# A store of 512 bytes a partition beside the first load of a split-GELU-multiply kernel

## The chip, the cores and the metric

The kernel runs on one core of a Trainium2 chip. The metric is the device time of one execution in microseconds (us); less is better. All runs quoted here are fast: one core, granted clock 1.0, no run over 1.5% above the fastest of its kernel. A ratio is the mean time of one kernel's fast runs over the mean of the other's in the same rounds, so it isn't quite the ratio of the medians that stand beside it. "Clear" below means that the 95% interval of that ratio leaves out 1.

## The reference

The input is 32 x 512 rows of 2048 float32 numbers. Each row is cut in two halves; GELU of the first half is multiplied by the second.

```python
def setup_inputs():
    batch, seq, dim = (32, 512, 2048)
    return {'x': np.random.randn(batch, seq, dim).astype(np.float32)}

def reference(x):
    half_dim = x.shape[-1] // 2
    x1, x2 = (x[..., :half_dim].copy(), x[..., half_dim:].copy())
    gelu_x1 = 0.5 * x1 * (1 + erf(x1 / np.sqrt(2)))
    return (gelu_x1 * x2).astype(np.float32)
```

That is 134.22 MB to read and 67.11 MB to write, and little arithmetic.

## The kernel before

Sixteen tiles of 128 partitions x 8 rows. A load brings 65,536 contiguous bytes to each partition, in one packet each (the trace has 2,048 packets of that size for 16 loads of 128 partitions); a store takes 32,768 from each (1,920 packets for the fifteen whole ones). Loads are issued on SyncE's queue, two tiles ahead; stores on ScalarE's queue, but for the last tile, whose store goes out in four pieces on SyncE's queue.

```python
    xpool = ctx.enter_context(tc.tile_pool(name="xpool", bufs=2))
    opool = ctx.enter_context(tc.tile_pool(name="opool", bufs=2))

    def load(i):
        x_tile = xpool.tile([P, R, dim], x.dtype, name="x_tile")
        nc.sync.dma_start(out=x_tile, in_=x_t[i])
        return x_tile

    ahead = [load(0), load(1)]
    for i in range(n_tiles):
        # ... GELU on ScalarE (in place), multiply on VectorE, row by row ...
            queue = nc.sync if last else nc.scalar
            queue.dma_start(out=o_t[i][:, rows, :], in_=o_tile[:, rows, :])
        if i + 2 < n_tiles:
            ahead.append(load(i + 2))
```

## Time and profile before

| | before |
|---|---|
| median time, first three runs | 472.24 us (471.88 to 472.30) |
| span of the profiled run | 470.3 us |
| VectorE / ScalarE busy | 31% / 26% |
| bytes moved, mean rate | 201.35 MB, 428 GB/s |

The lines of this profile, and how they are read, are in the prediction. Its result: some 6 us of the span are not explained by the bytes.

One source is used below that the summary page doesn't show: the trace's record of every DMA packet, with its queue, start, size and duration, though not which of the 16 engines carried it. From it I use one derived figure throughout, the **excess**. A packet of 65,536, 32,768 or 8,192 bytes normally takes 2.42, 1.213 or 0.309 us. What packets take beyond that (counted from 0.02 us on) is summed over a stretch and divided by 16; it is the mean time that an engine lost there. No view prints these records; every excess below was counted from them, in one trace of each kernel. "Stall" below means the excess at the first large store, 1.19 us in the kernel before.

### The profile page before, as it was taken

To read this page: it belongs to the slowest core of one execution; us is meant where nothing else is said; L and a number is where in the kernel's file an instruction comes from. 1 tells how busy PE (TensorE), PEld (TensorE's weight loads), DVE (VectorE), ACT (ScalarE), POOL (GpSimd) and SP (SyncE) were. 2 spreads that over 40 slices of the span, in tenths; PEclk is the share of its full clock that TensorE was granted. 3 is DMA by queue.
4 is the path that set the end of the run, shared out by engine and by line. 5 is a ranking of instruction groups with operands and counts; after the bars stand their busy time and mean duration, and the time that the engine had idled before them with its cause. 6 is when DMAs were issued, how large, how long until landed. Compare 5 with 4: busy or idle time off the path is not lost.

```text
span 470.3 us, 408 instructions
## 1 busy us (share of the span) xinstructions
DVE 146.7 (31%) x128; ACT 124.2 (26%) x129; POOL 0.2 (0%) x4
## 2 busy tenths in 40 slices
DVE  0070704307042070520606116060250702407034
ACT  1050605106050150601406024060330603206042
POOL 0000000000000000000000000000000000000000
DMA  8999999999999999999999999999999999999998
GB/s 357 446 446 382 429 443 424 463 404 443 426 446 421 443 415 449 413 443 424 457 429 435 438 438 415 426 438 435 440 440 418 449 438 435 424 443 432 418 410 351
DMA packets 5042, 201.35 MB, mean 428 GB/s; under 512 B 560, under 2 KB 560, under 8 KB 560
## 3 DMA queue, kind: packets, MB, share of 16 engines
q1 hardware_dynamic: 2880, 138.41, 68.4%
q10 hardware_dynamic: 2160, 62.92, 31.0%
q14 instruction: 2, 0.02, 0.0%
HBM read 134.22 MB, written 67.11 MB: 428 GB/s over the span
## 4 chain that ended last, share of the span: by engine, by line
DMA 81%; DVE 15%; ACT 2%; DVEq 0%; issue 0%; SPq 0%; ACTq 0%
DMA x_tile<-in_x_dram 81%; DVE o_tile L55 15%; ACT x_tile L52 2%; DVEq L90 0%; SPq L40 0%; ACTq L52 0%
## 5 line engine op out<-in xcount | busy, mean ns | idle before, releaser
L55 DVE TENSOR_TENSOR o_tile<-x_tile 128x1024 f32<-128x1024 f32 x128 | 146.7, 1218 | 316.8 <-ACT x_tile L52 316.8
L52 ACT ACTIVATE x_tile<-x_tile 128x1024 f32<-128x1024 f32 x128 | 122.9, 1042 | 336.0 <-DMA x_tile<-in_x_dram 336.0
L52 ACT ACT_TABLE_LOAD x1 | 1.3, 1283 | 0.7 <-PEq L79 0.7
L79 POOL MEMSET const-bfloat16-1.0<- 128x1 bf16 x1 | 0.1, 102 | 0.0
L79 POOL MEMSET const-uint8-127<- 128x1 uint8 x1 | 0.1, 102 | 0.0
L79 POOL MEMSET const-float32-1.0<- 128x1 f32 x1 | 0.1, 99 | 0.0
L79 POOL MEMSET const-float32-0.0<- 128x1 f32 x1 | 0.1, 98 | 0.2 <-issue 0.2
## 6 DMA issues: line engine op xcount, KB each, us to landing
out_dram<-o_tile ACTq DMA_DIRECT2D x15, 4096.0 KB, 39.4
out_dram<-o_tile SPq DMA_DIRECT2D x4, 1024.0 KB, 5.6
x_tile<-in_x_dram SPq DMA_DIRECT2D x16, 47.6
```

The source lines that it names most:

```text
L52: nc.scalar.activation(out=x_tile[:, r, :half], in_=x_tile[:, r, :half], func=GELU)
L55: nc.vector.tensor_mul(out=o_tile[:, r, :], in0=x_tile[:, r, :half], in1=x_tile[:, r, half:],)
L79: nc = _bacc.Bacc("TRN2", target_bir_lowering=False, num_devices=1)
```

## The change

The intent, as far as the code shows it, is to use ScalarE's queue once, early, so that the first real store finds it in use. The bytes written are dummies, and the last piece of the last store overwrites them.

```diff
+    first = ctx.enter_context(tc.tile_pool(name="first", bufs=1)).tile([P, 1, 128], out.dtype)
+    nc.vector.memset(first, 0.0)
+    nc.scalar.dma_start(out=o_t[n_tiles - 1][:, R - 1 :, half - 128 :], in_=first)
 
     ahead = [load(0), load(1)]
```

## The prediction

> **What bounds the kernel now.** I read the page first: busy shares, then the 40 slices, then the bytes.
>
> ```profile
> span 470.3 us, 408 instructions
> ...
> DVE 146.7 (31%) x128; ACT 124.2 (26%) x129; POOL 0.2 (0%) x4
> ...
> DMA  8999999999999999999999999999999999999998
> GB/s 357 446 446 382 429 443 424 463 404 443 426 446 421 443 415 449 413 443 424 457 429 435 438 438 415 426 438 435 440 440 418 449 438 435 424 443 432 418 410 351
> ...
> HBM read 134.22 MB, written 67.11 MB: 428 GB/s over the span
> ```
>
> No compute engine passes 31%, while the DMA row is at 9 in all but its first and last slice. The 16 DMA engines are the bound, and the bytes are given by the problem (134.22 MB in, 67.11 MB out). Next I read the chain that ended last:
>
> ```profile
> 1.16 45.96 DMA x_tile<-in_x_dram
> ...
> 57.44 47.69 DMA x_tile<-in_x_dram
> ...
> 115.50 47.63 DMA x_tile<-in_x_dram
> ...
> 173.50 47.63 DMA x_tile<-in_x_dram
> ...
> 405.50 47.65 DMA x_tile<-in_x_dram
> ```
>
> The columns are start, duration, what. Each link is a load's wait plus one tile's compute, and the links start exactly 58.0 us apart (57.44, 115.50, 173.50). Two tiles are 2 x (8.39 + 4.19) = 25.17 MB, and 25.17 MB / 58.0 us is 434 GB/s. So the compute inside each link is not what paces it: loads are queued two deep, and the transfers run through it. At that rate all 201.33 MB take 464.0 us. The span is 470.3, so everything that can be gained without moving fewer bytes is some 6 us, 1.3%. That alone almost excludes "faster by over 2%".
>
> Where are these 6 us? By the DMA queue's record of single packets, the first starts at 1.75 us and the last store's completions end at 469.0: 1.75 + 1.3 us lie outside, about 3.2 us inside. I looked for stretches under 434 GB/s in the view of engine time by stretch (stretch, length, busy us of DVE, ACT, POOL, clock, DMA share, GB/s):
>
> ```profile
> 34.00:41.60 7.60, 0.00 (x0) 0.00 (x0) 0.00 (x0) 1.00 1.00 366
> 41.60:57.40 15.80, 9.16 (x8) 7.68 (x8) 0.00 (x0) 1.00 1.01 438
> 57.40:86.40 29.00, 9.11 (x9) 7.68 (x8) 0.00 (x0) 1.00 1.00 434
> ...
> 458.00:469.00 11.00, 5.49 (x5) 2.91 (x4) 0.00 (x0) 1.00 0.92 379
> ```
>
> The first line is the interesting one. From 34 us the engines are fully occupied (share 1.00) and move 366 GB/s: they lose (1 - 366/434) x 7.6 = 1.19 us. It comes right behind the first store, issued on ScalarE's queue at 32.93. The packet records agree: a 65,536-byte load packet takes 2.42 us everywhere, but 23 of them between 34.1 and 39.0 us take 2.98 to 3.60, an excess of 18.8 us in sum, 1.17 us for each of 16 engines. The second store, at 57.44, and those after it show nothing of the kind. Something in the first store costs 1.17 us, once; this is evidently what the change aims at. Two other slow places stand beside it. The first packet of each engine takes 0.1 to 1.0 us more than 2.42 (mean 0.57). At 458 us, where stores begin on the load queue after it has run dry, 8 engines' first packets take 0.7 to 1.1 us more.
>
> [...]here load packets (65,536 bytes) and store packets (32,768 bytes) do alternate, so the added store takes time from the first load and not from idle hardware. [...]the added store has just 512 a partition, and no transfer of that size is in this trace. [...]
>
> **The change part by part.** It removes nothing. It adds:
>
> 1. A memset of 128x1x128 f32 on VectorE, at about 0.75 us. VectorE is idle until 23.7, so even a few tenths of a microsecond cost nothing.
> 2. One DMA issue on ScalarE. An issue there takes 0.36 us (median in the store's line). ScalarE has only its table load (0.72 to 2.00 us) to do before 22.64, so even with the wait for the memset this is hidden:
>
> ```profile
> 0.72 1.28 ACT L52 ACT_TABLE_LOAD   x1 [0.72 <-PEq L79]
> 0.73 0.86 SPq L40 DMA_DIRECT2D x_tile<-in_x_dram  x2
> ```
>
> 3. Its bytes: 128 x 512 = 65.5 KB, 8 packets for each engine. From the records, 8,192 bytes take 309 ns and 32,768 take 1,213, so a byte costs 0.0368 ns and a packet 8 ns besides; 512 bytes then take an estimated 27 ns, eight of them 0.21 us. These are engine time on the bound, so they count in full: +0.2 us.
> 4. A dependence: the last quarter of the last store overwrites these bytes and must wait for the small store. That one is issued at 463.5 us and the small one is done by about 20 (one small packet behind each of the first load's eight packets of 2.42 us). Cost 0. The shift of semaphores by one transfer shouldn't add a wait either, for neighbours keep their distance.
> 5. What it moves: if the 1.17 us is a cost of the queue's first store on each engine, the real first store no longer pays it, but the small one does, at 2 to 6 us, while the first load runs. There it costs the bound as much as before, except for what hides behind the first load's own slow start (mean 0.57 us of excess in the same first packets). The small store's descriptors should reach the engines roughly 1 us after its issue (as the first load's did: issue 0.73, first packet 1.75), hence at about 2.0 us, just as those slow packets are under way.
>
> Sum if it warms: -1.17 + 0.21 + a repeated stall of 0 to 1.17. That is -0.96 to +0.21, middle -0.4 us.
>
> **The rivals.** First rival: the stall isn't first use but the waking of an empty queue. For it: the second store came while the first was still under way (the first landed at 66.7, the second was issued at 57.44), so the trace has no second waking of ScalarE's queue; and the load queue, sixteen loads old, shows slow packets at 458 when it wakes. Against it: those eight engines had probably just finished everything else, so an empty pipeline explains them as well. If it holds, the small store is over by 20 us, the queue is empty at 32.9, the old stall stays and a second one may come: +0.2 to +1.4, middle +0.8 us.
>
> Second rival: it's the turn from reading alone to reading and writing. Then 64 KB of writes at 3 us train nothing, the stall at 34 stays, and only the 0.2 us of packets is added, with perhaps tenths for eight small turns an engine: +0.2 to +0.6.
>
> Third rival: a wait. If the program were to order the large stores behind the small one, because they go to the same tensor, the first store at 32.9 would still find it landed at 20. No effect. Only if such a wait sat on SyncE ahead of the first load, or if ScalarE held its table load until after 22 us, would it show; both are placed on other queues or over long before.
>
> **Range and chances.** I give warming 0.5, the two rivals that keep the stall 0.25 each. The mean is 0.5 x (-0.4) + 0.25 x 0.8 + 0.25 x 0.4 = +0.1 us, so I predict no more than a nudge: 472.24 + 0.1 - 0.2 for the chance of fully hiding the repeated stall is 472.1. The edges: the best case is -0.96, the worst +1.4, and the three runs before span 0.42 us. So 470.9 to 473.5 should hold it 8 times in 10. Two per cent are 9.4 us, over one and a half times all that is lost today; I leave 0.01 for faster and 0.01 for slower (a wait I overlooked), 0.98 for the same.
>
> **What would show each step.** In the changed profile: a row for the small store among the DMA issues, x1, 64 KB, with 15 to 20 us to landing (packet-by-packet alternation; a landing of 3 us would refute that). The stretch from 34.0 to 41.6 us at about 434 GB/s and the load packets there at 2.42 us if warming holds; still 366 if a rival does. The first load's packets at 2 to 6 us lengthened if the stall moved. The chain's links still 58.0 us apart. The landing of the second load, 47.13 before, shows the balance by itself: 46.2 to 47.3 with warming, 47.3 to 48.5 without; the end of the span should move by the same amount. The prediction is wrong if the links' spacing changes, if a wait on the small store shows up in the chain, or if the end moves by over 1.5 us.

That 434 GB/s can't be passed, on which the 6 us rest, is an estimate from this trace, which held that rate from link to link, 58.0 us at a time; it was not shown.

## The result, and the profile after

After: 472.38 us median (472.26 to 472.67, 4 runs). Before: 472.27 us (471.88 to 472.57, 4 runs). The ratio is 1.0004, with a 95% interval of 0.9986 to 1.0021: the same.

The page of the changed kernel, its busy shares and bytes:

```profile
span 470.6 us, 411 instructions
...
DVE 146.9 (31%) x129; ACT 124.2 (26%) x129; POOL 0.2 (0%) x4
...
HBM read 134.22 MB, written 67.17 MB: 428 GB/s over the span
```

There are three instructions more and 0.06 MB more written; the busy times agree within 0.2 us. The start of the timeline (start, duration, engine, line, what, and in brackets the idle time before it):

```profile
0.73 57.39 SPq L40 DMA_DIRECT2D x_tile<-in_x_dram  x4
0.83 0.17 DVE L45 MEMSET first<- 128x128 f32 x1 [0.83 <-PEq L84]
1.02 0.42 ACTq L46 DMA_DIRECT2D out_dram<-first  x1
1.47 1.28 ACT L57 ACT_TABLE_LOAD   x1 [1.47 <-DVE first L45]
22.93 7.68 ACT L57 ACTIVATE x_tile<-x_tile 128x1024 f32<-128x1024 f32 x8 [20.18 <-DMA x_tile<-in_x_dram]
```

The memset, the issue and the delayed table load are over by 2.75 us and ScalarE then waits 20.18 us for the first load, so these three are hidden. But the first load is in at 22.93; before, ScalarE could start at 22.64. That is +0.29 us on the bound. The chain that ended last (start, duration, what) carries it on:

```profile
1.17 46.31 DMA x_tile<-in_x_dram
...
57.79 47.68 DMA x_tile<-in_x_dram
...
115.84 47.64 DMA x_tile<-in_x_dram
...
405.85 47.64 DMA x_tile<-in_x_dram
```

The second load ends at 47.48 (1.17 + 46.31) in place of 47.13, the next links start 0.35 us later than before (57.79 against 57.44), the spacing is still 58.0 us, and the last link is 0.35 us later too (405.85 against 405.50). So what happened, happened before 58 us and wasn't given back. These are single traces, and 0.35 us is less than the 0.7 us over which the four runs of the kernel before spread.

Did the first store's stall go away? The view by stretch seems to say yes and then no:

```profile
34.00:41.60 7.60, 0.00 (x0) 0.00 (x0) 0.00 (x0) 1.00 1.16 431
34.30:41.90 7.60, 0.00 (x0) 0.00 (x0) 0.00 (x0) 1.00 0.97 354
```

Both lines are of the changed kernel. The first is the stretch that read 366 GB/s before; it now reads 431. Moved by 0.3 us, the amount by which everything came later, it reads 354. This view books a packet's bytes where the packet starts; packets are 2.4 us long and start in bunches, so an edge that cuts a bunch was worth 77 GB/s here. A DMA share of 1.16, over 1, is the sign of it. The packet records settle it: between 34.2 and 38.8 us, 19 load packets took 3.06 to 3.65 us in place of 2.42, an excess of 1.22 us an engine, against 1.17 (1.19 by the same count) before. The stall stayed in full.

The small store itself, in the view of DMA issues (what, queue, times, KB each, us from issue to landing):

```profile
out_dram<-first ACTq DMA_DIRECT2D x1, 64.0 KB, 24.3
```

Its packets are in the records: 128 of 512 bytes at 27 ns, alternating with the load's, the first at 7.21 us. Eight for each engine make 0.21 us, and the first packets of the first load have 0.66 us of excess in place of 0.57. 0.21 + 0.09 is the 0.3 us by which the first load is late. But the 0.09 is within chance: in the runs below whose first packets meet nothing new (e4_s7, e10_skew32 to e13_skew_ports) the same excess is 0.60 to 0.76.

### The profile page after: what moved, and what is told of

Read it like the earlier page. It is cut to its first block, busy times and chain, and to the rows that moved or that the text cites. A ratio compares the mean times of both kernels' runs of the same rounds, so it can differ in the third digit from the quotient of the medians.

```text
span 470.6 us, 411 instructions
## 1 busy us (share of the span) xinstructions
DVE 146.9 (31%) x129; ACT 124.2 (26%) x129; POOL 0.2 (0%) x4
## 4 chain that ended last, share of the span: by engine, by line
DMA 81%; DVE 15%; ACT 2%; DVEq 0%; issue 0%; SPq 0%; ACTq 0%
DMA x_tile<-in_x_dram 81%; DVE o_tile L60 15%; ACT x_tile L57 2%; DVEq L95 0%; SPq L40 0%; ACTq L57 0%
## 6 DMA issues: line engine op xcount, KB each, us to landing
out_dram<-first ACTq DMA_DIRECT2D x1, 64.0 KB, 24.3
```

## The experiments

Four theories were tested. (The expectations also say "ring", for the queue of one issuing engine.) **W**: the stall is the waking of an empty store queue. **T**: it is the turn from reading alone to reading with large stores. **F**, later **C**: it is paid once a run, by the first large store (F), or by whatever first crowds the engines (C). "Crowds" means here that something lengthens their packets, as the column "early" below counts it. **P**: it is the shock of 16 engines in step meeting large stores at once. The theory of the prediction, that a small first store warms the queue, had fallen with the profile after.

The table has all twelve runs beside the two kernels. "Early" is the excess an engine between 4 and 30 us, "first store" that between 30 and 60 us, where the first full-size store meets the loads.

| run | early | first store | median us | before in its rounds |
|---|---|---|---|---|
| before | 0.00 | 1.19 | 472.27 | |
| the change | 0.00 | 1.22 | 472.38 | 472.27 |
| e1_late | 0.03 | 1.13 | 473.59 | 472.37 |
| e2_bridge | 0.00 | 0.86 | 472.26 | 472.37 |
| e3_big | 1.37 | 0.00 | 473.64 | 472.37 |
| e4_s7 | 0.00 | 1.42 | 473.40 | 472.37 |
| e5_2k | 0.02 | 1.21 | 473.41 | 472.31 |
| e6_skew | 0.62 (and 2.59 before 4 us) | 0.00 | 474.88 | 472.31 |
| e7_sync | 0.88 | 0.11 | 473.65 | 472.31 |
| e8_8k | 0.05 | 1.27 | 472.88 | 472.31 |
| e10_skew32 | 3.36 | 0.00 | 475.84 | 472.39 |
| e11_drain | 0.00 | 1.31 | 473.14 | 472.39 |
| e12_half | 0.00 | 0.94 | 471.84 | 472.39 |
| e13_skew_ports | 0.00 | 1.33 | 473.48 | 472.48 |

All gave correct results.

**e1_late: the small store in the middle of the first load.**

```diff
-    nc.vector.memset(first, 0.0)
+    for _ in range(60):
+        nc.vector.memset(first, 0.0)
```

> The small store as in the change, but behind 60 memsets of its tile, so that it is issued some 7 to 10 us into the first load, when load packets run at their steady 2.42 us and no slow start hides anything. Theory W (waking an empty store queue stalls the loads): load packets lengthened by some 1.2 us for each engine just after the small store's descriptors arrive, the first load lands 1.2 us later than 22.93, and the old stall stays at 34 us; the time goes up by 1.0 to 1.3 us against the change. Theory T (the stall is the turn from reading alone to large stores beside the reads): no load packet lengthened at 10 us, the stall at 34 stays, first load lands at 22.9, the time is that of the change within 0.3 us.

The 60 memsets took longer than I thought; the small store was issued at 16.26 us. From its timeline:

```profile
0.82 15.41 DVE L46 MEMSET first<- 128x128 f32 x60 [0.82 <-PEq L85]
16.26 0.38 ACTq L47 DMA_DIRECT2D out_dram<-first  x1
22.69 7.68 ACT L58 ACTIVATE x_tile<-x_tile 128x1024 f32<-128x1024 f32 x8 [4.74 <-DMA x_tile<-in_x_dram]
```

The first load is in by 22.69 (before: 22.64), and no load packet was lengthened when the small store came. So small packets woke the queue without a loss (0.03 us of excess between 4 and 30 us), even where no slow start could hide it. More than that: the small store's last completions came at 38.7 to 40.1 us, so the queue was not empty when the first real store was issued at 32.98, and the stall came all the same, 1.13 us an engine between 38.7 and 40.1, the moment before the large packets began. W is out as the cause of this stall. The time is clearly longer (ratio 1.0026, 1.0011 to 1.0041), by 1.2 us against the change. That is the time W asked for, but not for W's reason, since neither the lengthened load packets nor the late first load came; T asked for no more than 0.3 us. The longer time shows at the end: 15 of the 16 last completions came by 468.75 us, earlier than before (469.00), and one at 470.50. With the extra instructions there was a third fetch of 8,192 bytes of program, at 27.09, and a load packet starting at 27.39 took 0.53 us more; the two fetches of the kernel before, at 180.09 and 198.32, each came with one lengthened load packet in the same way (0.24 and 0.53 us). That the late engine is the one that fetches is argued, not shown.

**e2_bridge: the small store lasts until the real one comes.**

```diff
-    first = ... .tile([P, 1, 128], out.dtype)
+    first = ... .tile([P, 2, 128], out.dtype)
-    nc.scalar.dma_start(out=o_t[n_tiles - 1][:, R - 1 :, half - 128 :], in_=first)
+    nc.scalar.dma_start(out=o_t[n_tiles - 1][:, R - 2 :, half - 128 :], in_=first)
```

> The small store has two pieces of 512 bytes a partition, 16 packets an engine in place of 8; at one packet behind each load packet of 2.42 us it lasts from 7 to some 45 us, so that the store queue is not empty when the first real store is issued at 33.2. Theory W: no stall of load packets at 34 to 39 us, none when the first large packets come at about 45 either; second load lands at about 46.7 (47.50 less 1.2, plus 0.2 for 8 more packets, with fewer large store packets ahead of it sooner still); end about 0.8 to 1.0 us earlier than the change, about 471.5. Theory T: the stall comes all the same, at 44 to 48 us, when the first large packets run; time 472.6, 0.2 over the change.

Small packets ran from 7.1 to 41.8 us, about one in every 2.4 us on each engine; the stall came at 41.3 to 41.8 us, on all 16 engines at once, 0.86 us each, as the first large packets were next. This is against W again. The time was the same (0.9998, 0.9983 to 1.0013).

**e3_big: one full-size packet an engine, early.**

```diff
-    first = ... .tile([P, 1, 128], out.dtype)
-    nc.vector.memset(first, 0.0)
-    nc.scalar.dma_start(out=o_t[n_tiles - 1][:, R - 1 :, half - 128 :], in_=first)
+    first = opool.tile([P, R, half], out.dtype, name="o_tile")
+    nc.vector.memset(first[:16], 0.0)
+    nc.scalar.dma_start(out=o_t[n_tiles - 1][:16], in_=first[:16])
```

> In place of the small store one full-size packet an engine: 16 partitions of 32,768 bytes, issued at about 9 to 10 us after a memset of 16x8192. It adds 0.52 MB, 1.21 us for each engine. Theory W and theory T both: load packets lengthened by about 1.2 us an engine at 10 to 15 us, and again at 34 to 39 us, as the queue is empty (W) and the engines read alone (T) again by then; first load lands at 22.6 + 1.2 + 1.2 = 25.0; end 2.4 us over before, 474.6. Theory F (only the first full-size store in the program pays): stall at 10 to 15, none at 34 to 39; end 1.2 us over before, 473.4.

Here the stall at the first real store is gone, while 1.37 us an engine were lost at 12 to 17 us. The time, 473.64, is what F asked for (473.4) and not what W and T asked for (474.6). By the view of stretches, from 29 to 49 us, this kernel first, then before:

```profile
29.00:49.00 20.00, 6.56 (x6) 4.67 (x6) 0.00 (x0) 1.00 1.03 444
```
```profile
29.00:49.00 20.00, 4.67 (x5) 3.18 (x4) 0.00 (x0) 1.00 1.02 416
```

(The view's weakness told above applies; the records have no load packet over 2.44 us in this stretch of e3_big.) T is out too in its plain form: the engines read alone from 20 us on and turned to mixing at 39 without a loss.

The records show that the early loss has another form than the stall, so it isn't shown to be the stall moved forward. In the ten kernels that stall (0.86 us or more in the table), load packets are lengthened, and at least 16 of them start before the first large store packet: in the kernel before 16 of 23, from 34.09 us, while the first store packet starts at 37.27; in e1_late and e2_bridge all 16. The first store packets themselves take their usual time. In e3_big the early store's own packets are lengthened (1.64 to 2.98 us in place of 1.213, 1.25 of the 1.37 us), and load packets hardly (0.13).

**e4_s7: ScalarE's queue runs dry in mid-run.** The kernel before, with one line changed:

```diff
-            queue = nc.sync if last else nc.scalar
+            queue = nc.sync if last or i == 7 else nc.scalar
```

> The kernel before (no small store), with the eighth tile's store issued on SyncE's queue in place of ScalarE's. ScalarE's queue then runs dry for some 20 us in the middle of the run, and is woken by the ninth tile's store; SyncE's queue goes from load packets to store packets and back in one ring without ever being empty. Theory W: load packets lengthened, about 1.2 us an engine, once more when the ninth tile's store arrives, and none where the eighth's begins; end about 1.2 us over before. Theory T: a stall where the eighth tile's store begins to run after a stretch of reading alone, if there is one, and none or the same at the ninth. Theory F: no stall besides the one at 34, time as before within 0.5 us unless the order of transfers in SyncE's queue delays a load.

On SyncE's queue the engines went from load packets straight to 10 us of store packets alone, at 245.3 us, and every one took 1.213 us, give or take 0.02: that turn cost nothing. When the ninth tile's store then woke ScalarE's queue, load packets between 258 and 265 us were lengthened by 0.5 us an engine, less than half of what W asked, and 0.1 came at 297. By the stretch from 258 to 267 us of this kernel (the kernel before has 419 GB/s there, and the view's weakness applies):

```profile
258.00:267.00 9.00, 0.00 (x0) 0.00 (x0) 0.00 (x0) 1.00 0.97 397
```

So something does come back here, in part, and it comes when a dry queue gets a large store, as W asks. A strict "once a run" isn't right either. The time is clearly longer (1.0022, 1.0007 to 1.0037), by 1.0 us where W asked for 1.2 and F for at most 0.5.

**e5_2k and e8_8k: how large must the early store be?** The change with 2,048 bytes a partition, and one packet of 8,192 bytes for each engine from 16 partitions:

```diff
 e5_2k
-    first = ... .tile([P, 1, 128], out.dtype)
+    first = ... .tile([P, 1, 512], out.dtype)
-    nc.scalar.dma_start(out=o_t[n_tiles - 1][:, R - 1 :, half - 128 :], in_=first)
+    nc.scalar.dma_start(out=o_t[n_tiles - 1][:, R - 1 :, half - 512 :], in_=first)
 e8_8k (against e3_big)
-    nc.vector.memset(first[:16], 0.0)
-    nc.scalar.dma_start(out=o_t[n_tiles - 1][:16], in_=first[:16])
+    nc.vector.memset(first[:16, :2], 0.0)
+    nc.scalar.dma_start(out=o_t[n_tiles - 1][:16, :2], in_=first[:16, :2])
```

> The change with 2,048 bytes a partition in place of 512: eight packets of an estimated 83 ns for each engine (0.0368 ns a byte and 8 ns), 0.67 us in all, one behind each packet of the first load. Theory F (the first large store pays the stall, once): if 2,048 bytes are large enough, load packets near 7 us are lengthened and those at 34 to 39 us are not; if not, the stall of 1.2 us an engine stays at 34 to 39. Time 472.4 + 0.46 = 472.9 if the stall only moves or stays. Theory P (the stall is the shock of 16 engines in step turning to large stores at once): stays at 34 to 39, same time.

> One early store packet of 8,192 bytes an engine on ScalarE's queue (16 partitions, memset of 16x2048, issue at about 4.5 us), 0.31 us of engine time. Theory F: an excess of 0.3 to 1.2 us an engine at 6 to 10 us and what is missing from 1.2 at 34 to 39, so that the sum stays about 1.2; time 472.3 + 0.3 = 472.6. Theory P: whatever happens at 6 to 10, the excess at 34 to 39 goes down as the first load's completions spread more.

Neither crowded the engines early (0.02 and 0.05) and neither took anything off the stall (1.21 and 1.27). For e8_8k no share of the 1.2 moved to the front, which is a miss of F as I had put it; nor did the excess at 34 to 39 us go down, which is a miss of P. Its time isn't clearly longer (1.0008, 0.9993 to 1.0023). e5_2k took 1.1 us more than before (1.0021, 1.0004 to 1.0038) where 0.6 was expected; its last completions are spread from 468.99 to 470.29.

**e6_skew and e7_sync.** No early store but an extra load of 8 partitions in front of the first; and the early full-size store on SyncE's queue:

```diff
 e6_skew (against before)
+    first = opool.tile([P, R, half], out.dtype, name="o_tile")
+    nc.sync.dma_start(
+        out=first[:8].rearrange("p (a b) d -> p a (b d)", b=2), in_=x_t[0][:8, : R // 2]
+    )
 
 e7_sync (against before)
-    ahead = [load(0), load(1)]
+    ahead = [load(0)]
+    first = opool.tile([P, R, half], out.dtype, name="o_tile")
+    nc.vector.memset(first[:16], 0.0)
+    nc.sync.dma_start(out=o_t[n_tiles - 1][:16], in_=first[:16])
+    ahead.append(load(1))
```

> No early store; in its place an extra load of 8 partitions x 32,768 bytes in front of the first load, which keeps 8 of the 16 engines busy 1.21 us longer, so that the engines no longer reach the first store in step (the completions of the first load spread over about 1.8 us in place of 0.6). Theory P: the excess at 34 to 39 us falls to half or less of the 1.2 us an engine. Theory F: it stays at 1.1 to 1.3 us an engine. The end is set by the 8 engines with more work: 472.3 + 1.2 = 473.5 with F, 472.5 to 472.9 with P.

> The full-size early store of 16 partitions x 32,768 bytes is put on SyncE's queue, between the first and the second load, so one store packet an engine runs at about 22 us in the ring of the loads. Theory F with the cost belonging to the engine or to the memory, not to the ring: an excess of about 1.2 us an engine at 20 to 24 us, none at 34 to 39; time 473.6 as with the full-size store on ScalarE's queue. If the cost belongs to the first large use of ScalarE's ring: no excess or the same at 22, and again 1.2 at 34 to 39; time 473.6 to 474.8. Theory P: a stall at 22, as the engines are in step, and little at 34 to 39.

e6_skew took the stall away without any early store, which spoke for P and against F. But it had a defect: the extra load lost 2.6 us an engine of its own in the first microseconds (2.59 + 0.62, less the usual 0.6), which I had not asked for. e7_sync lost 0.88 at 19 to 24 us on the loads' queue, 0.64 of it on the early store's own packets, and left 0.11 at the first real store. In both runs the first use of ScalarE's queue went almost without loss (0.00 and 0.11 us). So the cost doesn't belong to the first use of that queue.

**e10_skew32 and e13_skew_ports: the skew alone.** Both put the extra load of 8 x 32,768 bytes between the first and the second load. They differ only in the partitions it is written to:

```diff
 e10_skew32 (against before)
-    ahead = [load(0), load(1)]
+    ahead = [load(0)]
+    extra = opool.tile([P, R, half], out.dtype, name="o_tile")
+    nc.sync.dma_start(
+        out=extra[:8, : 2 * 4].rearrange("p (a b) d -> p a (b d)", b=2),
+        in_=x_t[1][:8, :4],
+    )
+    ahead.append(load(1))
 
 e13_skew_ports (against e10_skew32)
-        out=extra[:8, : 2 * 4].rearrange("p (a b) d -> p a (b d)", b=2),
+        out=extra[0:32:4, : 2 * 4].rearrange("p (a b) d -> p a (b d)", b=2),
```

> No early store. An extra load of 8 partitions x 32,768 bytes on 8 of the 16 engines stands between the first and the second load, so that the start is untouched and those engines come to the first store 1.21 us behind the others. Theory P (the stall is the shock of engines in step turning to large stores at once): excess at 34 to 39 us at most 0.3 us an engine, in place of 1.2. Theory C (a cost paid once a run, by the first thing that upsets the start, which the misplaced extra load of the run before this may have paid with its 2.6 us of added excess in the first microseconds): 1.1 to 1.3 us an engine at 34 to 39. The end: 8 engines have 1.21 us more to do, so 472.3 with P (1.2 added, 1.2 saved), 473.5 with C.

> The extra load of 8 x 32,768 bytes between the first and the second load again, but written to partitions 0, 4, 8 ... 28 in place of 0 to 7. [...]extra packets at about 1.21 us, load packets at 2.42, and the 8 engines are simply 1.21 us behind the others. Then the run tells the two theories apart, for nothing but the skew is left. Theory P (engines in step): excess at 34 to 39 us at most 0.3 us an engine, end near 472.3. Theory C (a stall paid once a run, by whatever first crowds the engines: in all the runs without it at 34, something had crowded them before): 1.1 to 1.3 us an engine at 34 to 39, end near 473.5.

The stretch from 21.6 to 29 us, first of e10_skew32, then of e13_skew_ports:

```profile
21.60:29.00 7.40, 4.68 (x5) 5.76 (x7) 0.00 (x0) 1.00 1.13 292
```
```profile
21.60:29.00 7.40, 5.27 (x5) 6.36 (x7) 0.00 (x0) 1.00 1.06 461
```

With partitions 0 to 7, the eight extra packets took 3.0 to 4.0 us in place of 1.21, eight load packets that ran beside them 5.75 in place of 2.42, and the eight load packets behind the extra ones 3.07 to 3.95: 3.36 us an engine lost. With partitions 0, 4, ... 28 nothing was lost. The choice of the partitions written to is all that differs, and it made 3.36 against 0.00 us; by what way it does so was not shown. (The 461 GB/s of the second line is an edge through a bunch again.)

That nothing was lost in e13_skew_ports decides between P and C. Eight engines were 1.2 us behind, so the 16 were not in step; nothing else was disturbed (0.00 early); and the stall came in full: 1.33 us an engine. The time, 473.48 us, is C's 473.5 and not P's 472.3. P is out as it was put. Nor does a skew explain e6_skew: there the first load ended in two groups of engines 0.9 us apart, much as here, and the stall was gone. What separates the runs without the stall (e3_big, e6_skew, e7_sync, e10_skew32: 0.00 to 0.11) from all others (0.86 to 1.42) is that something had crowded the engines by at least 0.88 us before.

**e11_drain and e12_half.**

```diff
 e11_drain (against before)
-        if i + 2 < n_tiles:
+        if i == 7:
+            back = ctx.enter_context(tc.tile_pool(name="back", bufs=1)).tile([P, 1, 128], out.dtype)
+            nc.sync.dma_start(out=back, in_=o_t[7][:, R - 1 :, half - 128 :])
+            ahead.append(load(8))
+        if i != 6 and i + 2 < n_tiles:
             ahead.append(load(i + 2))
 e12_half (against before)
-        pieces = 4 if last else 1
+        pieces = 4 if last else 2 if i == 0 else 1
```

> The kernel before, but the ninth and tenth loads wait for the eighth store (by way of a small load that reads back its last bytes), so that all transfers run dry in the middle of the run and start again in step, in a kernel that has stored for 200 us. Theory P: once the ninth tile's store comes, some 33 us after the restart, load packets are lengthened again by 0.8 to 1.3 us an engine. Theory C and theory F (once a run): none there. The stall at 34 us is in both. The time goes up by the empty stretch, 10 to 40 us, and is not to be compared.

> No early store. The first tile's store alone is cut in two halves of 16,384 bytes a partition, the first issued after four of the eight rows, some 4.6 us sooner. The first packets that meet the loads are thus half as large, and there are two for each engine in the round where there was one. Theory P: the shock shrinks with the packet, an excess of 0.3 to 0.9 us an engine at 30 to 39 us, time 471.6 to 472.2. Theory F or C: 1.1 to 1.3 us in all, time 472.3 within 0.3. If the slower draining of the first store (16 packets behind 16 load packets) delays the third tile, 473 or more, and a new wait for it shows on VectorE near 76 us.

e11_drain failed as a test. The ninth and tenth loads depend on nothing but free buffers, so they were put ahead of the small read-back in SyncE's order, and only the eleventh came late: the first two were issued by 231.86 us, the read-back at 270.92, and the next load from 271.35, while the tenth was still under way (in at 279.2). So the transfers never ran dry. Some 0.05 us of excess was all that followed at 284 to 297 us. Whether a restart in mid-run brings the full stall back stays open.

e12_half is nominally the fastest, 471.84 us (471.67 to 472.94, 5 runs), but with a ratio of 0.9990 (0.9976 to 1.0003) it isn't shown to be faster. Its excess was 0.94 in all, most of it in two bites, 0.35 us at 31.5 and 0.53 at 41. C's "1.1 to 1.3 in all" missed. P's "0.3 to 0.9 at 30 to 39 us" held, with 0.40 there, and so did its time, though e13_skew_ports speaks against P. The bite at 41 us has no explanation. No version beats both kernels clearly.

## Why the prediction was right or wrong

**The time was right**: 472.38 us against 472.1 predicted, inside 470.9 to 473.5, and "same" had 0.98. It was right for its main reason, the bound: the whole slack was put at 6 us, and nothing in the change touches the 434 GB/s or the bytes. The links still are 58.0 us apart. That the middle came so close is luck: it is a mean over warming and its rivals, and the 0.2 us taken off "for the chance of fully hiding the repeated stall" was counted twice, since the middle of the warming branch (-0.4) already averages over that chance.

**Steps 1 and 2, memset and issue hidden: right.** 0.17 and 0.42 us, done before 2 us, with ScalarE waiting until 22.93.

**Step 3, 0.21 us of packets on the bound: right.** Packets of 512 bytes took 27 ns, as estimated, and the first load came 0.29 us later.

**Step 4, no wait for the overwritten bytes: right in effect, wrong in its times.** The chain shows no new wait, and the view of waits adds only the table load's for the memset (1.5 us) and the memset's own at the start (0.8). But the small store landed 24.3 us after its issue, at some 25 us, not by 20. I had put a small packet behind each of the first load's eight packets; they began only behind the second (7.21 us), so that the last ones ran at 21.8 to 22.6 us, behind the eighth, and their completions came at 24.3 to 25.0, behind the second load's first packets (21.9 to 22.6).

**Step 5, the stall moves to the front: wrong.** This was the term of -1.17 us that I gave a chance of one half. The measured change at the first store was +0.03 us (1.22 against 1.19), and the repeated stall at the front was at most 0.09 us of the "0 to 1.17". So a small store neither takes the cost off the first real one nor pays it itself. The time doesn't show this error: the warming branch's middle of -0.4 and the 0.35 of the chain are 0.75 us apart, and the runs of the kernel before spread over 0.7.

**The first rival, waking an empty queue: wrong for this stall**, by e1_late and e2_bridge, where the queue was not empty and the stall came (1.13 and 0.86 us). e4_s7's 0.5 us in mid-run leaves room for a smaller cost of waking a queue with a large store. The reading of the slow packets at 458 us (eight of 8,192 bytes took 0.99 to 1.39 us in place of 0.309) as engines that had just run empty wasn't tested and isn't shown.

**The second rival, the turn to mixed traffic: its sum was right, +0.2 to +0.6 against a measured 0.35 in the chain, its cause was not.** e3_big, e6_skew and e10_skew32 make the same turn without loss (0.00 us each).

**The check I had announced was poor.** "The stretch from 34.0 to 41.6 us at about 434 GB/s if warming holds; still 366 if a rival does" would have come out for warming, with 431, because an edge of the stretch cut through a bunch of packets. The reading before the change rests on the same view: the kernel before reads 414 GB/s from 33.7 to 41.3 us, 366 from 34.0 to 41.6 and 336 from 34.3 to 41.9. That the 366 gave 1.19 us, next to the packets' 1.17, was luck; the packets carry the point.

**What the stall is stays open.** Shown: it doesn't need an empty queue (1.13 us in e1_late, 0.86 in e2_bridge), nor 16 engines in step (1.33 in e13_skew_ports); neither the first use of ScalarE's queue nor the turn to mixed traffic brings it by itself (e6_skew and e10_skew32 have both, and 0.00 us); it falls on the load packets ahead of the first large store packets; stores of 512, 2,048 and 8,192 bytes a packet ahead of it don't pay it (1.22, 1.21 and 1.27 us stayed); and each of the four runs in which something crowded the engines earlier by 0.88 us or more did without it, or nearly (0.11 in e7_sync). That the crowding is the reason is argued from these four, not shown; all of them sent full-size packets to or from partitions 0 to 7 or 0 to 15 alone, so I can't separate "crowded" from "crowded by packets of these partitions". e4_s7's half stall in mid-run and e12_half's two bites fit none of the theories. And each of these four runs took longer than the kernel before, by 1.27 us (e3_big) or more, so none of them is a remedy.

## What to carry to other kernels

Where the loads in the chain are evenly spaced (here 58.0 us for two tiles, 434 GB/s), work out first what the whole slack at that rate is (here 6 us of 470); a change that takes away no bytes and doesn't raise the rate can't gain more than that, however good its mechanism. A dummy transfer put in to warm something up takes its place on the busy engines, here 0.21 us of 472 by its packets, and it warms nothing unless a trace shows the slow packets gone. Before you trust a rate over a few microseconds, shift the stretch by a fraction of a packet and read it again (here 0.3 us made 354 GB/s of 431).

## What else the packet records show

- The first packet of a store didn't get its turn right after the packet under way. In the changed kernel the small store, issued at 1.02 us, got its first packet in at 7.21, behind two packets of the first load; and the first full-size one, issued at 33.23, at 37.28.
- A packet of 512 bytes took 27 ns, 19 GB/s for an engine; 2,048 bytes (e5_2k) took 84 ns, 24; 65,536 bytes took 2.42 us, 27. So 512 bytes reached 70% of the rate of the large packets.
- Each of the 29 fetches of 8,192 bytes of program within the spans of these 14 traces was followed by one lengthened packet that starts 0.30 to 0.31 us after it, about the fetch's own 0.309 us: 28 load packets, longer by 0.24 to 0.56 us, and one store packet, by 0.35. Whether it is the next packet of the same engine is not shown; the records don't name the engine.
